# A hybrid transformer block on one core: the second tokens' first output projection placed in attention's last steps, operands formed in PSUM

## Chip, core and metric

The kernel runs on one core of a Trainium2 chip. The metric is the device time of one execution in microseconds. The span in a profile is the time from its first to its last instruction.

## The reference

One block over 1024 tokens of width 1024. An RMSNorm and one input projection feed a pooling mixer (512 columns) and differential attention (four heads of two score maps each, block-causal). Their outputs are put side by side, projected by `w_o` and added to x. A second RMSNorm feeds a gated MLP (up projection to 2 x 2816 columns, causal convolution of width 3 over the tokens, silu(gate) x value, down projection), which is added, and a last RMSNorm follows.

```python
mix = jnp.concatenate([pool_out, attn_out], axis=-1) @ w_o[l]
x = x + mix
h = rmsnorm(x, norm_ffn_g[l])
u = causal_dwconv(h @ w_up[l], conv_w[l], conv_b[l])
gate, val = jnp.split(u, 2, axis=-1)
x = x + (jax.nn.silu(gate) * val) @ w_down[l]
...
return rmsnorm(x, norm_final_g)
```

## The kernel before

Tokens lie in eight tiles of 128 (`tt` 0 to 7). The first tokens are tiles 0 to 3, the second tokens 4 to 7. Every float32 operand of a large product is split into a high part, rounded by ScalarE (`split`, L86), and a low part, the rest, by VectorE or GpSimd (L87). A product is then three matmuls, `mm3` (L79 to L81): high by high, high by low, low by high.

The start. `col` holds columns of constants, among them the norm's gain. For each of eight k tiles a weight tile `wv` and a tile of the transposed input `xT` are loaded by the SP queue and split, and the value projection `pv` is formed in all eight PSUM banks.

Attention. `att_steps` makes a list of steps, 32 query tiles and 8 steps to finish, and `merge` weaves units from the list `fill` between them, among them the output projection of the first tokens. A fifth entry of a unit in `fill` names the step at which it comes at the latest.

The output projection. `wo_part(hf, part, n)` loads and splits weights for one token half, one half of the rows of `w_o` (`part` 0 holds the pooled columns, `part` 1 the attention's) and one half of the output columns. `wo_unit(tt, part, n, w)` is twelve matmuls into a bank `po` and one addition into `X1[tt]` on VectorE.

The second norm. `norm2a(tt)` squares and sums `X1[tt]` on ScalarE, makes the inverse root on GpSimd, and multiplies on VectorE by it and by the gain `gb`, which SP loads, into `xn`. `norm2b(tt)` transposes `xn` on TensorE into a PSUM tile `t` of two banks: `q1` (first four k tiles) and `q2`.

The up projection follows Winograd's form of Strassen's product, seven half-size products in place of eight. The right operands are blocks of the transposed tokens: B11 and B21 (first tokens), B22 (second tokens' `q2`), and the sums T1 = B12 - B11, T2 = B22 - T1, T3 = B22 - B12, T4 = B21 - T2, with B12 = `q1` of the second tokens. The left operands are weight blocks a11 to a22 and their sums S1 to S4, made on GpSimd from loads. `operand` gives their places, `osplit` splits into them. The first four units of the up projection (`AHEAD`) have their products P1 (with B11) and P2 (with B21) done ahead, while the second tokens' operands are made; `ug`, by `c11`, is the addition on VectorE that follows P2. Then the loop `up` begins with P6, the product of S2 and T2, then Z, of S1 and T1. Later pages of the program, the convolution and the down projection, have an order written out by hand for all engines (from `manual_schedule`); before that a scheduler at build time orders each engine's instructions by their priority in the code, and `tc.high_priority()` puts some of them forward.

The end. The last product group is finished tile by tile: `evac` adds it to X on VectorE, `last1` squares on ScalarE, applies the gain on VectorE, forms the mean on GpSimd (`mean`) and the inverse root there (`power`), and `last2` multiplies one half on VectorE and one on ScalarE and stores each half.

Of the kernel before, what the change touches and what calls it, by code (L numbers as in the profile page):

```python
# [50 lines left out]
def block_kernel(ctx, tc, x, xT, pos, wv, wqk, wp, wo, wup, wdn, cols, invf, rcnt, gffn, gfin,  # L51
# [58 lines left out]
    nc.sync.dma_start(out=col[:, 0:16], in_=cols[:, 0:16])  # L110
# [33 lines left out]
    pv = []  # L144
    for i in range(2):
        s = psS(f"pv{i}")
        pv += [s[:, 0:H], s[:, H:T]]
    for i in range(4):
        pv.append(psB(f"pv{4 + i}"))
# [485 lines left out]
    def norm2b(tt):  # L635
# [11 lines left out]
        t1, t4 = fb["B11", tt - 4], fb["B21", tt - 4]  # L647
        sub = ALU.subtract
# [12 lines left out]
        fb["B22", tt] = b22  # L661
# [15 lines left out]
    w00 = wo_part(1, 0, 0, "s")  # L677
# [242 lines left out]
    for u in us[:AHEAD]:  # L920
# [7 lines left out]
        if u.n == 0:
            norm2b(7)
# [313 lines left out]
```

## Time and profile before

| what | us |
|---|---|
| median of three runs | 1042.85 |
| lowest of them | 1039.86 |
| the profiled execution | 1039.9 |
| its span | 1038.1 |
| TensorE busy in the span | 1009.8 |
| VectorE busy | 765.1 |
| ScalarE busy | 508.0 |
| GpSimd busy | 246.5 |

One of the three runs took 2449.37 us and tells nothing about the kernel. The profile's times count from the span's start. PE is TensorE, PEld its weight loads, DVE VectorE, ACT ScalarE, POOL GpSimd, SP the queue that issues the transfers. In a row of a timeline the bracket holds the idle time of the engine just before the instruction and what ended it.

### The profile page before, as it was taken

The numbers are of one execution on the slowest core, as the hardware profiler recorded it, in microseconds if no ns is written. First come the engines' busy times: TensorE is split into PE (matmuls) and PEld (weight loads), VectorE is DVE, ScalarE is ACT, GpSimd is POOL, SyncE is SP. The second block draws the span as 40 slices with busy tenths as digits, with TensorE's granted clock in tenths as the row PEclk, the third lists the DMA queues.
The fourth block names the chain that finished last, engine by engine and source line by source line (L and its number), as shares of the span: only waits on it lengthen the run. The fifth ranks groups of instructions, "written<-read, shape, count | busy, mean of one in ns | idle before, by whom it ended". The sixth has DMA issues, their size and how long they took to land.

```text
span 1038.1 us, 13407 instructions
## 1 busy us (share of the span) xinstructions
PE 1009.8 (97%) x4612; PEld 834.6 (80%) x4612; DVE 765.1 (74%) x1169; ACT 508.0 (49%) x884; POOL 246.5 (24%) x232
## 2 busy tenths in 40 slices
PE   8999999998998999999999999999999999999997
PEld 6888888886887887778888888888888788888885
DVE  6466777989775869688876776776776878958774
ACT  6732554447554545353544545445445453544553
POOL 0000112223221137543333332432432000000221
PEclk9999999999999999999999999999999999999999
DMA  9627543324325412223331431432321897533342
GB/s 313 240 87 257 194 163 112 109 70 148 102 81 186 150 61 72 101 92 112 132 117 56 140 113 51 143 112 72 132 102 41 297 389 266 173 111 101 120 145 81
DMA packets 67971, 143.88 MB, mean 139 GB/s; under 512 B 8512, under 2 KB 9664, under 8 KB 67904
## 3 DMA queue, kind: packets, MB, share of 16 engines
q1 hardware_dynamic: 67904, 143.03, 39.9%
q8 instruction: 36, 0.59, 0.2%
q14 instruction: 31, 0.25, 0.1%
HBM read 105.78 MB, written 37.22 MB: 138 GB/s over the span
## 4 chain that ended last, share of the span: by engine, by line
PE 73%; DVE 7%; issue 2%; ACT 2%; DMA 1%; POOL 1%; SPq 1%; POOLq 0%; DVEq 0%; ACTq 0%
PE P L81 8%; PE P L79 8%; PE P L80 8%; PE Z L79 3%; PE x L80 3%; PE x L81 3%; PE Z L81 3%; PE Z L80 3%; PE x L79 3%; PE dP L79 3%; PE dP L81 3%; PE dP L80 3%; PE po L81 3%; PE po L79 3%; PE po L80 3%; PE sc L386 3%
## 5 line engine op out<-in xcount | busy, mean ns | idle before, releaser
L403 POOL TENSOR_SCALAR e<-e,sm 128x128 f32<-128x128 f32 (+7 forms) x32 | 29.9, 936 | 175.8 <-DMA k<-tsk 69.5
L735 POOL TENSOR_TENSOR S<-wa,wa 128x512 f32<-128x512 f32 x44 | 64.8, 1495 | 0.5 <-DMA wa<-in_wup 0.5
L399 ACT ACTIVATE e<-sc,mx 128x128 f32<-128x128 f32 (+7 forms) x64 | 47.2, 742 | 32.2 <-DVE mx L389 16.7
L1034 POOL TENSOR_SCALAR s<-s 128x1 f32<-128x1 f32 x12 | 9.4, 786 | 212.8 <-ACT sq0None L1031 167.5
L753 DVE SCALAR_TENSOR_TENSOR o<-ug,col,o 128x1023 f32<-128x1023 f32 (+1 forms) x44 | 56.4, 1282 | 0.0
L753 DVE SCALAR_TENSOR_TENSOR o<-uv,col,o 128x1023 f32<-128x1023 f32 (+1 forms) x44 | 56.3, 1280 | 0.0
L735 POOL TENSOR_TENSOR S<-S,wa 128x512 f32<-128x512 f32 x22 | 28.3, 1287 | 73.8 <-DVE a227l L87 4.8
L860 ACT COPY u<-P 128x512 f32<-128x512 f32 x18 | 10.6, 590 | 69.2 <-PE P L81 69.2
L386 PE MATMUL sc<-K,Q 128*128 128x512 f32 (+3 forms) x192 | 42.6, 351 | 0.7 <-ACT e L399 0.7
L735 POOL TENSOR_TENSOR S<-wa,S 128x512 f32<-128x512 f32 x22 | 28.5, 1295 | 50.5 <-issue 50.4
L386 PEld LDWEIGHTS sc<-K,Q 128*128 128x128 f32 x192 | 32.4, 189 | 6.0 <-ACT e L399 1.2
L421 ACT COPY at<-tp 128x512 f32<-128x512 f32 (+3 forms) x48 | 21.6, 483 | 28.8 <-PE tp L417 28.8
L748 ACT ACTIVATE o<-ug,col 128x1024 f32<-128x1024 f32 x22 | 26.7, 1212 | 18.2 <-DVE ug L912 18.2
L840 ACT COPY u<-P 128x512 f32<-128x512 f32 x18 | 10.6, 590 | 49.9 <-PE P L81 49.9
L433 PE MATMUL O<-at,V 128*128 128x256 f32 (+1 forms) x160 | 34.0, 358 | 0.0
L433 PEld LDWEIGHTS O<-at,V 128*128 128x128 f32 x160 | 29.8, 190 | 4.0
L816 DVE TENSOR_TENSOR ac<-o,g 128x1024 f32<-128x1024 f32 x22 | 26.9, 1225 | 7.9 <-ACT g L814 7.9
L389 DVE TENSOR_REDUCE mx<-sc 128x1 f32<-128x640 f32 (+3 forms) x32 | 32.3, 1016 | 0.4
L564 DVE TENSOR_TENSOR X<-X,po 128x512 f32<-128x512 f32 x32 | 21.7, 683 | 13.6 <-PE po L81 13.5
L748 ACT ACTIVATE o<-uv,col 128x1024 f32<-128x1024 f32 x22 | 26.7, 1213 | 9.1 <-DVE uv L892 9.1
L814 ACT ACTIVATE g<-o 128x1024 f32<-128x1024 f32 x22 | 22.7, 1030 | 13.6 <-DVE o L753 13.5
L879 ACT COPY s<-P 128x512 f32<-128x512 f32 x18 | 10.6, 590 | 32.8 <-PE P L81 32.8
(2451 smaller groups left out, 3479.9 us busy)
## 6 DMA issues: line engine op xcount, KB each, us to landing
wa<-in_wup SPq DMA_DIRECT2D x88, 256.0 KB, 3.2
S<-s SPq DMA_DIRECT2D x22, 512.0 KB, 2.9
arP<-S SPq DMA_DIRECT2D x44, 256.0 KB, 2.6
arP<-A SPq DMA_DIRECT2D x33, 256.0 KB, 4.5
Q<-q SPq DMA_DIRECT2D x64, 128.0 KB, 2.8
A<-ac SPq DMA_DIRECT2D x11, 512.0 KB, 2.8
xs<-in_x SPq DMA_DIRECT2D x8, 512.0 KB, 8.0
K<-k SPq DMA_DIRECT2D x8, 512.0 KB, 4.9
```

Of the source, the lines that this page charges most:

```text
L79: mm(dst, lhi, rhi, start=first, stop=False, skip_group_check=more)
L80: mm(dst, lhi, rlo, start=False, stop=False, skip_group_check=more)
L81: mm(dst, llo, rhi, start=False, stop=last, skip_group_check=more)
L386: mm(sc[:, k0:k1], qst[h, grp][n * 2 + hl][:, qc], kst[h][n][:, k0:k1], start=hl == 0, stop=hl == 1)
L389: nc.vector.tensor_reduce(out=nmx[:, n:n + 1], in_=sc[:, 0:L], axis=AX.X, op=ALU.max, negate=True)
L399: nc.scalar.activation(ee[n], scs[n][:, 0:L], AF.Exp, bias=nmx[:, n:n + 1], accum_out=sums[:, n:n + 1])
L403: nc.gpsimd.tensor_scalar(out=e1, in0=e1, scalar1=sums[:, 3:4], scalar2=1.0, op0=ALU.mult, op1=ALU.mult)
L433: mm(O[:, c0:256], V[j][:, h * P:(h + 1) * P], at[:, j, c0:256], start=j == 0, stop=j == nj - 1)
L735: pool(out=t, in0=getattr(u, x), in1=getattr(u, y), op=op)
L748: nc.scalar.activation(o, src, AF.Identity, bias=col[:, cc + 3:cc + 4], scale=col[:, cc + 2:cc + 3])
L753: nc.vector.scalar_tensor_tensor(out=o[:, d:T], in0=src[:, 0:T - d], scalar=col[:, cc + 2 - d:cc + 3 - d], in1=o[:, d:T], op0=ALU.mult, op ...
L816: tens(out=p.act, in0=p.o1, in1=g, op=ALU.mult)
```

## The change

Four things are changed.

1. At the start `col` and the first quarter of the first `xT` tile are issued by ScalarE instead of SP, the second `xT` tile comes in halves, and TensorE first multiplies a tile of zeros seven times into a bank that the first real product overwrites.
2. The second tokens' first output projection (`part` 0, first column half) becomes four units of `fill`, due at the steps 35 to 38 of 40, with its weights and the loads of the second tokens' X in the first of them. Before, it was written behind the attention, each unit ahead of a `norm2a`.
3. For the second tokens `norm2b` no longer makes T1 and T2 in SBUF. VectorE writes T1 over `q1` and T2 over `q2`; B22 is split from `q2` at once, not later by another loop; T4's subtraction moves from GpSimd to VectorE. The `norm2b` of tiles 4 to 7 come at other places.
4. At the end the mean is no longer a GpSimd instruction: its factor is in the square's scale, and VectorE adds the constant. `last2` splits a tile at column 640, not 512, and stores it whole.

```diff
 col = cst.tile([P, 192], F32, name="col")
-nc.sync.dma_start(out=col[:, 0:16], in_=cols[:, 0:16])
+nc.scalar.dma_start(out=col[:, 0:16], in_=cols[:, 0:16])
...
+zero = st("lo", "zero")
+nc.vector.memset(zero, 0.0)
+zr = st("hi", "zeror", dt=F32R)
+nc.vector.tensor_copy(out=zr, in_=zero)
+for i in range(7):
+    mm(pv[7], zr[:, 0:P], zr, start=True, stop=True)
...
+    t = st("E", f"xT{kt}")
+    w = 256 if kt == 0 else H if kt == 1 else T
+    if kt == 0:
+        nc.scalar.dma_start(out=t[:, 0:w], in_=xT[0:P, 0:w])
...
+w00 = []
+def wo_first(tt):
+    if not w00:
+        load_x1(1)
+        w00.extend(wo_part(1, 0, 0, "s"))
+    wo_unit(tt, 0, 0, w00)
+    yield
+fill += [(wo_first(4 + j), 0.0, 35 + j, 0.0, 35 + j) for j in range(4)]
...
-t1, t4 = fb["B11", tt - 4], fb["B21", tt - 4]
-nc.vector.tensor_tensor(out=t1, in0=q1, in1=t1, op=sub)
+b1, t4 = fb["B11", tt - 4], fb["B21", tt - 4]
+sub, tens = ALU.subtract, nc.vector.tensor_tensor
 b22 = st("Q", f"B22f{tt}", [P, 4, P])
 nc.scalar.copy(out=b22, in_=q2)
-t2 = st("T", f"T2f{tt}", [P, 4, P])
-nc.gpsimd.tensor_tensor(out=t2, in0=b22, in1=t1, op=sub)
 t3 = st("Q", f"T3f{tt}", [P, 4, P])
-nc.vector.tensor_tensor(out=t3, in0=b22, in1=q1, op=sub)
-osplit("T1", tt, t1)
-osplit("T2", tt, t2)
-osplit("T3", tt, t3)
-nc.gpsimd.tensor_tensor(out=t4, in0=t4, in1=t2, op=sub)
+tens(out=t3, in0=b22, in1=q1, op=sub)
+tens(out=q1, in0=q1, in1=b1, op=sub)
+osplit("B22", tt, q2)
+tens(out=q2, in0=b22, in1=q1, op=sub)
+tens(out=t4, in0=t4, in1=q2, op=sub)
+osplit("T2", tt, q2)
+osplit("T1", tt, q1)
+osplit("T3", tt, t3, None)
 osplit("T4", tt, t4, nc.gpsimd)
-fb["B22", tt] = b22
...
-w00 = wo_part(1, 0, 0, "s")
...
-for tt in range(4, 8):
-    wo_unit(tt, 0, 0, w00)
-    if tt < 6:
-        norm2a(tt - 4)
+norm2a(0)
+norm2a(1)
...
-    nc.scalar.activation(junk[:, cs], X[tt][:, cs], AF.Square, accum_out=...)
+    nc.scalar.activation(junk[:, cs], X[tt][:, cs], AF.Square, scale=1.0 / 32, accum_out=...)
...
-    mean(s[:, 3:4], s[:, 0:1], s[:, 2:3])
+    tens(out=s[:, 3:4], in0=s[:, 0:1], in1=s[:, 2:3], op=add)
...
-    for n in range(2):
-        emit(tt, halves[n])
+    m = 640
...
+    emit(tt, slice(0, T))
```

The order of the instructions is the scheduler's, and changes at the start, between the end of attention and P6, and at the end; SP's is the same but for the start and the stores at the end, and from P6's first matmul to the last product TensorE's is the same.

On ScalarE at the start of the program before (`g08` are gains of the attention's norm, made from `col`):

```order
L338 ACT_TABLE_LOAD
L338 ACTIVATE g08_483<-col_69 128x4
L86 CAST wv0h_75<-wv0r_73 128x512
L89 ACTIVATE hTh0_71<-xT0_79,col_69 128x256 x4
L86 CAST wv1h_94<-wv1r_92 128x512
```

and now:

```order
L110 DMA col_69<-in_cols 128x16
L139 DMA xT0_90<-in_xT 128x256
L86 ACT_TABLE_LOAD
L86 CAST wv0h_94<-wv0r_92 128x512
L349 ACTIVATE g08_497<-col_69 128x4
L89 ACTIVATE hTh0_88<-xT0_90,col_69 128x256 x4
L86 CAST wv1h_112<-wv1r_110 128x512
```

The two issues come first, and `g08` moved behind the cast of the first weight tile.

On TensorE where attention ends, before (`rb` and `so` are small steps of the heads' norm, `t20` and `t21` the transposes of token tiles 0 and 1, `po004` the product of tile 4):

```order
L456 MATMUL rb23_3169<-ident_168,rs23_3099 128x128 x2
L638 MATMUL t20_3423<-ident_168,xn0_3263 128x128 x4
L638 MATMUL t21_3467<-ident_168,xn1_3286 128x128 x4
...
L444 MATMUL so33_3175<-ones_173,sq33_3158 128x1 x2
L456 MATMUL rb32_3183<-ident_168,rs32_3164 128x128 x2
L456 MATMUL rb33_3187<-ident_168,rs33_3178 128x128 x2
L79 MATMUL po004_3249<-wo100h_3205,cat010_2293 128x512
L80 MATMUL po004_3249<-wo100l_3206,cat010_2293 128x512
L81 MATMUL po004_3249<-wo100h_3205,cat011_2294 128x512
```

and now:

```order
L467 MATMUL rb23_3183<-ident_188,rs23_3113 128x128 x2
L79 MATMUL po004_3221<-wo100h_3199,cat010_2307 128x512
L80 MATMUL po004_3221<-wo100l_3200,cat010_2307 128x512
...
L81 MATMUL po004_3221<-wo103h_3217,cat011_2308 128x512
L658 MATMUL t20_3437<-ident_188,xn0_3319 128x128 x4
L658 MATMUL t21_3481<-ident_188,xn1_3328 128x128 x3
L79 MATMUL po005_3235<-wo100h_3199,cat010_2307 128x512
...
L455 MATMUL so33_3249<-ones_193,sq33_3172 128x1 x2
L658 MATMUL t20_3437<-ident_188,xn0_3319 128x128 x4
L658 MATMUL t21_3481<-ident_188,xn1_3328 128x128 x5
L467 MATMUL rb32_3257<-ident_188,rs32_3178 128x128 x2
L79 MATMUL po006_3261<-wo100h_3199,cat010_2307 128x512
```

Twelve matmuls of tile 4, and then of tile 5, moved ahead of the transposes and of the small steps that stood in front of them.

On VectorE at the last token tile's operands, before (`ug...` is the addition after P2 of one unit, `S20l` the low part of the first unit's S2):

```order
L649 TENSOR_TENSOR B11f3_3547<-t27_3824,B11f3_3547 128x512
L655 TENSOR_TENSOR T3f7_3838<-B22f7_3834,t27_3824 128x512
L87 TENSOR_TENSOR T110_3646<-B11f3_3547,T100_3645 128x4x128
L742 TENSOR_TENSOR ug11_3905<-P211_3892,s111_3890 128x512
L87 TENSOR_TENSOR T310_3655<-T3f7_3838,T300_3653 128x2x128
L87 TENSOR_TENSOR T311_3656<-T3f7_3838,T301_3654 128x2x128
L87 TENSOR_TENSOR T210_3650<-T2f7_3836,T200_3649 128x4x128
L742 TENSOR_TENSOR ug1_3935<-P21_3922,s11_3920 128x512
L742 TENSOR_TENSOR ug12_3965<-P212_3952,s112_3950 128x512
L87 TENSOR_TENSOR S20l_3968<-S20_3863,S20h_3967 128x512
```

and now (L674 writes T1 into `t27`, L676 T2, L677 is T4):

```order
L673 TENSOR_TENSOR T3f7_3869<-B22f7_3867,t27_3858 128x512
L674 TENSOR_TENSOR t27_3858<-t27_3858,B11f3_3561 128x512
L87 TENSOR_TENSOR T310_3687<-T3f7_3869,T300_3685 128x2x128
L87 TENSOR_TENSOR T311_3688<-T3f7_3869,T301_3686 128x2x128
L87 TENSOR_TENSOR B2210_3672<-t27_3858,B2200_3671 128x4x128
L676 TENSOR_TENSOR t27_3858<-B22f7_3867,t27_3858 128x512
L677 TENSOR_TENSOR B21f3_3565<-B21f3_3565,t27_3858 128x512
L759 TENSOR_TENSOR ug12_3975<-P212_3962,s112_3960 128x512
L87 TENSOR_TENSOR T210_3678<-t27_3858,T200_3677 128x4x128
L87 TENSOR_TENSOR S20l_3978<-S20_3913,S20h_3977 128x512
L87 TENSOR_TENSOR S10l_3982<-S10_3909,S10h_3981 128x512
L87 TENSOR_TENSOR T110_3682<-t27_3858,T100_3681 128x4x128
```

The two subtractions for T2 and T4 and B22's split came into VectorE's row; T1's low part (`T110`) moved from the third place to behind S2's and S1's, and T2's (`T210`) stands behind `ug12`, no longer ahead of it.

## Rows read from the trace of the kernel before

**Rows 1.** page, part 1: busy us, share of the span, instructions of each engine
```profile
PE 1009.8 (97%) x4612; PEld 834.6 (80%) x4612; DVE 765.1 (74%) x1169; ACT 508.0 (49%) x884; POOL 246.5 (24%) x232
```

**Rows 2.** table by stage: stretch; its us; busy us (x) of five engines; clock; DMA
```profile
330.00:340.00 10.00, 6.41 (x36) 4.63 (x35) 7.46 (x19) 5.97 (x13) 1.81 (x3) 0.89 0.64 215
...
340.00:350.00 10.00, 10.00 (x43) 8.18 (x42) 9.53 (x16) 7.24 (x14) 3.10 (x4) 0.94 0.42 152
...
400.00:410.00 10.00, 7.80 (x34) 6.10 (x33) 9.35 (x15) 4.97 (x11) 4.89 (x4) 0.98 0.31 106
...
410.00:420.00 10.00, 7.63 (x26) 5.54 (x25) 6.98 (x6) 3.91 (x7) 9.12 (x7) 0.85 0.27 92
...
480.00:600.00 120.00, 120.00 (x531) 99.36 (x530) 86.73 (x101) 58.72 (x89) 44.81 (x33) 1.00 0.31 106
...
1020.00:1038.10 18.10, 10.69 (x48) 8.51 (x46) 7.20 (x12) 5.47 (x12) 3.46 (x8) 0.89 0.31 116
```

**Rows 3.** timeline, start of the span: start us, us, engine, line, operation, idle before
```profile
0.73 0.39 SPq L110 DMA_DIRECT2D col<-in_cols  x1
...
1.17 0.42 SPq L96 DMA_DIRECT2D wv0r<-in_wv  x1
...
2.39 0.21 ACT L338 ACTIVATE g<-col 128x4 f32<-128x4 f32 x1 [0.39 <-DMA col<-in_cols]
...
4.04 0.62 ACT L86 CAST wv0h<-wv0r 128x512 fp32r<-128x512 f32 x1 [1.45 <-DMA wv0r<-in_wv]
...
5.12 0.79 PE L79 MATMUL pv<-wv0h,hTh 128*128 128x512 f32 x1 [5.12 <-ACT hTh L89]
...
9.56 0.63 PE L79 MATMUL pv<-wv0h,hTh 128*128 128x512 f32 x1
...
9.98 0.48 PE L80 MATMUL pv<-wv0l,hTh 128*128 128x512 f32 x1
```

**Rows 4.** timeline around the end of attention, TensorE and VectorE
```profile
330.52 0.41 PE L456 MATMUL rb<-ident,rs 128*128 128x128 f32 x2
...
331.71 1.42 DVE L617 SCALAR_TENSOR_TENSOR xn<-X,r,gbhi 128x512 f32<-128x512 f32 x2 [3.31 <-DMA gbhi<-in_gffn]
...
338.46 0.78 PE L79 MATMUL po<-wo100h,cat 128*128 128x512 f32 x1
...
350.79 0.39 PE L79 MATMUL po<-woh,cat 128*128 128x512 f32 x1
```

**Rows 5.** instructions by form, 378 to 420 us: count | busy, mean ns | idle before, releaser
```profile
L87 DVE TENSOR_TENSOR T<-T2f,T 128x512 fp32r<-128x512 f32 x4 | 4.3, 1074 | 0.0
...
L655 DVE TENSOR_TENSOR T3f<-B22f,t 128x512 f32<-128x512 f32 x4 | 2.7, 682 | 1.3 <-ACT B22f L651 1.3
...
L653 POOL TENSOR_TENSOR T2f<-B22f,B11f 128x512 f32<-128x512 f32 x4 | 5.9, 1470 | 10.1 <-ACT B22f L651 10.1
...
L651 ACT COPY B22f<-t 128x512 f32<-128x512 f32 x4 | 2.4, 588 | 13.2 <-DVE B11f L649 13.2
```

**Rows 6.** timeline, operands of the last token tile and what follows on TensorE
```profile
398.83 0.66 PE L638 MATMUL t<-ident,xn 128*128 128x128 f32 x4 [0.35 <-DVE xn L617]
...
405.18 0.68 DVE L649 TENSOR_TENSOR B11f<-t,B11f 128x512 f32<-128x512 f32 x1
...
408.05 0.50 PE L79 MATMUL P<-B,aa120h 128*128 128x512 f32 x1 [2.20 <-ACT s L924]
...
417.26 0.50 PE L79 MATMUL P<-T,S20h 128*128 128x512 f32 x1 [1.85 <-ACT S20h L86]
```

**Rows 7.** timeline of the last token tile; then DMA issues: count, KB, us to landing
```profile
1032.33 0.34 POOL L1034 TENSOR_SCALAR s<-s 128x1 f32<-128x1 f32 x1 [1.07 <-ACT sq L1031]
...
1033.34 0.72 ACT L1084 ACTIVATE of<-of,s 128x512 f32<-128x512 f32 x1 [0.49 <-POOL s L1037]
...
out_dram<-of SPq DMA_DIRECT2D x4, 512.0 KB, 2.9
out_dram<-of SPq DMA_DIRECT2D x8, 256.0 KB, 2.2
```

More of the change, by code (lines that the diff above doesn't have):

```diff
@@ L109, in block_kernel @@
     col = cst.tile([P, 192], F32, name="col")
-    nc.sync.dma_start(out=col[:, 0:16], in_=cols[:, 0:16])
+    nc.scalar.dma_start(out=col[:, 0:16], in_=cols[:, 0:16])
+    pv = []
+    for i in range(2):
+        s = psS(f"pv{i}")
+        pv += [s[:, 0:H], s[:, H:T]]
+    for i in range(4):
+        pv.append(psB(f"pv{4 + i}"))
+    zero = st("lo", "zero")
[4 more added lines that the diff above has]
+        mm(pv[7], zr[:, 0:P], zr, start=True, stop=True)
     hT = [[None] * NK, [None] * NK]
@@ L121, in block_kernel @@
         hT[1][kt] = b[:, kt % 2, :]
+        t = st("E", f"xT{kt}")
+        w = 256 if kt == 0 else H if kt == 1 else T
+        if kt == 0:
+            nc.scalar.dma_start(out=t[:, 0:w], in_=xT[0:P, 0:w])
         wvs.append(weight(wv[:, kt, :], f"wv{kt}"))
-        t = st("E", f"xT{kt}")
-        w = 256 if kt == 0 else T
         for c0 in range(0, T, w):
             c = slice(c0, c0 + w)
-            nc.sync.dma_start(out=t[:, c], in_=xT[kt * P:(kt + 1) * P, c])
+            if kt or c0:
+                nc.sync.dma_start(out=t[:, c], in_=xT[kt * P:(kt + 1) * P, c])
             split(t[:, c], hT[0][kt][:, c], hT[1][kt][:, c], col[:, kt:kt + 1])
@@ L141, in block_kernel @@
     nc.sync.dma_start(out=rcn, in_=rcnt.partition_broadcast(P))
[L144 to L149, printed above, removed]
     for kt in range(NK):
@@ L695, in block_kernel @@
         wo_unit(tt, 1, 0, w10)
+        if tt > 5:
+            norm2b(tt - 2)
         wo_unit(tt, 1, 1, w11)
         norm2a(tt)
-        if tt > 4:
-            norm2b(tt - 1)
     acts, opd, U = {}, {}, {}
@@ L924, in block_kernel @@
         nc.scalar.copy(out=u.s1, in_=x)
+        if u.n < 2:
+            norm2b(6 + u.n)
         y = psB(f"P2{u.f}")
@@ L927, in block_kernel @@
         c11(u, y)
-        if u.n == 0:
-            norm2b(7)
+        if u.n == 1:
+            u = us[0]
             up_load(u, "a21", "a22", "a11", "a12")
@@ L932, in block_kernel @@
                 up_sum(u, k)
-            for tt in range(4, 8):
-                osplit("B22", tt, fb["B22", tt], nc.gpsimd if tt % 2 else None)
     up_split(us[0], "S2")
@@ L1030, in square @@
         junk = psS(f"sq{tt}{n}")
-        nc.scalar.activation(junk[:, cs], X[tt][:, cs], AF.Square, accum_out=s3[tt][:, n or 0:(n or 0) + 1])
-    def mean(dst, src, plus):
-        nc.gpsimd.tensor_scalar(out=dst, in0=src, scalar1=1.0 / D, scalar2=plus, op0=ALU.mult, op1=ALU.add)
+        nc.scalar.activation(junk[:, cs], X[tt][:, cs], AF.Square, scale=1.0 / 32, accum_out=s3[tt][:, n or 0:(n or 0) + 1])
     def power(s):
@@ L1049, in upper @@
         elif step == 1:
-            mean(s[:, 3:4], s[:, 0:1], EPS)
+            nc.vector.tensor_scalar_add(out=s[:, 3:4], in0=s[:, 0:1], scalar1=EPS)
             power(s[:, 3:4])
@@ L1070, in lower @@
         elif step == 1:
-            mean(s[:, 2:3], s[:, 1:2], EPS)
+            nc.vector.tensor_scalar_add(out=s[:, 2:3], in0=s[:, 1:2], scalar1=EPS)
             gain(tt, 1)
@@ L1082, in last2 @@
         o, s = fin[tt], s3[tt]
-        nc.vector.tensor_scalar_mul(out=o[:, 0:H], in0=o[:, 0:H], scalar1=s[:, 3:4])
-        nc.scalar.activation(o[:, H:T], o[:, H:T], AF.Copy, scale=s[:, 3:4])
-        for n in range(2):
-            emit(tt, halves[n])
+        m = 640
+        nc.vector.tensor_scalar_mul(out=o[:, 0:m], in0=o[:, 0:m], scalar1=s[:, 3:4])
+        nc.scalar.activation(o[:, m:T], o[:, m:T], AF.Copy, scale=s[:, 3:4])
+        emit(tt, slice(0, T))
     todo = {}
```

2 lines of the change are left out of this document (removed).

## The prediction

> **What bounds the kernel now.** The line of engines [rows 1] comes first: TensorE is busy for 1009.8 us of 1038.1 and no other engine reaches 75%. So an edit away from TensorE is worth only what it takes out of the 28.3 us in which TensorE stands still, or out of the stretches where its clock is halved. The table by stage [rows 2] says where these are: from 480 to 600 us TensorE is busy 120.00 of 120.00 (531 matmuls, 0.226 us each) and nothing there can be won by overlap. The losses that the diff touches are four. Ahead of the first matmul 5.12 us pass [rows 3]. Around 330 to 350 us, where attention ends and the output projection of the second tokens begins (I call it the join), 3.59 us are idle and the granted clock is 0.89 and 0.94, which is another 0.11 x 10 + 0.06 x 10 = 1.7 us of full-speed time. Around 400 to 420 us, where the up projection's operands are made, 2.20 + 2.37 us are idle and the clock is 0.98 and 0.85, another 0.2 + 1.5 = 1.7 us. In the last stretch TensorE is busy 10.69 of 18.10 us, so 7.4 us follow its last matmul. The whole loss in reach is 5.1 + 5.3 + 6.3 + 7.4 us plus a slow start, and I take the four places in turn. The sum is made against the profiled execution's 1039.9 us, which is the lowest of the three times shown and 2.95 us under their median.
>
> **The start.** The chain is: SP issues `col` at 0.73 and `wv0r` at 1.17; the cast of `wv0r` begins at 4.04, 2.87 us after its issue; hTh follows and the first matmul starts at 5.12 [rows 3]. With `col` and the first piece of xT issued by ScalarE, `wv0r` takes SP's first place, 0.44 us earlier. But the new order on ScalarE puts the small g08 activation (0.21 us) between that cast and hTh, where it stood ahead of the cast before; and ScalarE's two issues come ahead of its table load, which still ends well before the weights land. So the first real matmul moves by 0.44 - 0.21 = 0.2 us, to 4.9. The larger part is the clock. The matmuls that start at 9.56 and 9.98 are 0.42 us apart, against 0.226 us later: the array starts at its lower level (1.2 GHz) although this column prints 1.00 there, and it stays there for about 4.9 us from the first matmul. Eleven matmuls start in that time, each 0.2 us too long. The seven products of zeros need a memset and a cast of 128x512 on VectorE, which does nothing else before 4 us; I estimate that they begin at 1.8 us and last 7 x 0.43 = 3.0 us, so they end where the real work begins and cost nothing. If the rise again comes 4.9 us after the first product, at 6.7, four real matmuls are slow instead of eleven: 7 x 0.2 = 1.4. Together **1.6 us**. Ends: 0.2 if the zeros don't raise the clock, 2.4 if no real matmul is slow. Data keeps up, since xT's second block is cut into halves and the next weights are issued two places earlier on SP.
>
> The start's clock has its page too: the Trainium skill (TensorE: Matmul & The Clock Gate, Part 1: The HAM clock gate) says that the phase of the activity watch is free, so that the number of slow matmuls at a start differs from run to run. No run here shows that; by it the term could be anything between its two ends, and the sum would move by about 1 us.
>
> **The join.** TensorE makes rb at 330.52 and then wants the transposes of xn, which VectorE can't form until gbhi has landed (its idle 3.31 us, until 331.71) [rows 4]; small steps that wait for each other follow, the first product of the second tokens starts at 338.46, already at the half clock (0.63 us), and the products with the second column half start at 350.79. The new order puts the twelve products of token tile 4 directly behind rb, those of tile 5 behind seven transposes, and the norm's small steps between them. A group of twelve takes 12 x 0.226 = 2.7 us, more than the time from rb to the end of VectorE's wait, and their weights are the ones loaded before the join. SP's order is the same on both sides there, so gbhi lands no later. What takes the wait's place: each group's PSUM buffer is freed by VectorE's addition, and VectorE holds the splits of `wor` in the same order; following it row by row I find tile 7's group waiting at worst 0.7 us for the addition of tile 5. From rb's end (330.93) to 350.79 are 19.9 us, in which stand 48 products (10.9 us) and, as I estimate, 2.3 us of transposes and small ones: 6.7 us over. The windows give 5.3. I take 6.2, the middle of the two rounded up, less the 0.7 us of new wait: **5.5 us** (4.0 to 6.3).
>
> Costed at nothing: the second tokens' X loads (same place on SP), and the last head's `cat`, now split some 10 us after rb but still about 2.5 us ahead of its first product; if that cover is gone, the excess falls on TensorE.
>
> **The operands.** What changes hands for each of the four token tiles: T2f, the update of B21f and half of B22's low parts leave GpSimd: 4 + 4 + 2 instructions, the shortest kind of which has a mean of 1470 ns [rows 5], so about 15 us. VectorE takes them at some 0.68 us, the mean of T3f, which reads PSUM as they do: 4 x 0.68 + 4 x 0.68 + 2 x 0.68 = 6.8 us more. In return the T2 and T1 splits, 1074 ns from SBUF now, would be at T3f's 0.68: 8 x 0.39 = 3.2 us less. The in-place PSUM results have no row; I take T3f's price, with 0.6 and 1.1 as ends. Before, VectorE came to the last tile at 405.18, some 6 us after its transposes (398.83), and from there came the idle spells: 2.20 us before 408.05, where a product waits for ScalarE, and 1.85 us before 417.26 [rows 6]. With less slowed work I get VectorE to the last tile some 2 us after its transposes.
>
> The transposes of tile 7 now stand later on TensorE, 27 matmuls (6.1 us) ahead of the product that needs T2. VectorE's row for tile 7 is T3f, q1, two half splits, B22, q2, T4 (about 4.5 us with the 2 us of lag and some contention: 7 to 8), then ug12, which waits for the last of those 27 matmuls, and only then T2's low part and S20l, another 2 x 0.68. So the wait at P6 doesn't vanish; I put it at 2.8 us. Old loss 6.3, new 2.8, leaves **3.5 us** (0 to 5). A new wait that is queued too: the t buffers are held until T1 is split, so the transposes of tiles 6 and 7, and all matmuls behind them, wait for VectorE's splits of tiles 4 and 5; I find 3 us or more of cover.
>
> ScalarE's copy of B22f stood 13.2 us in four times behind VectorE's subtraction on the other half of the same PSUM tile [rows 5]: the two engines take turns on it. The Trainium skill (PSUM — Partial Sum Buffer, PSUM bank collisions raise a hardware error) has a rule for this: two engines may not use one bank at a time and must be ordered. That speaks against forming more in PSUM: copy, T3f and q1, cast, split, q2 and T4, cast, split, cast, split become one chain of turns, 7 x 0.68 + 0.59 + 3 x 0.62 = 7.2 us a tile. After the last transposes T2 would then be ready after 5.9 us and T1 after 7.2; TensorE wants them 6.1 and 8.8 us after. By the rule the sum stays within 1 us of mine, as long as VectorE isn't behind.
>
> **The end.** Four instructions follow each last addition; the GpSimd step at 1032.33 (0.34 us) becomes a small VectorE addition and the last ScalarE multiplication (0.72 us at 1033.34) becomes 384 wide [rows 7]: 0.3 + 0.1 us, and one issue less. Against it one 512 KB store lands in 2.9 us where 256 KB take 2.2, and VectorE now multiplies tile 6 after that addition. **0.3 us** (-0.5 to 0.9).
>
> **Sum.** 1.6 + 5.5 + 3.5 + 0.3 = 10.9; 1039.9 - 10.9 = **1029.0 us**. Between the stages TensorE is full and its order is unchanged, so a shift passes through.
>
> **Rivals.**
> - Operand stage bound by VectorE: its share is already 9.35 of 10 us at 400 to 410 us [rows 2]. If splits there stay at 1.07 us, the wait at P6 grows to 5 us or more, the clock falls again (1.7), and nothing of the 3.5 is won: 1039.9 - 7.4 = 1032.5. For it: 13 VectorE instructions a tile. Against: T3f's 682 ns beside a busy GpSimd. Chance 0.2.
> - Zeros don't warm the array: the change does not do there what it seems to. 1039.9 - 9.5 = 1030.4. Chance 0.1.
> - Everything at its good end (2.4 + 6.3 + 5 + 0.9): 1025.3. Chance 0.07.
> - Slower than before: PSUM results in place cost VectorE far more than T3f. There are 28 such instructions (7 a tile) in one queue, ahead of ug and S20l, which TensorE waits for. Cover and gain are 3 + 11 us, so it decides from 0.68 + 14/28 = 1.2 us each; at 1.4 us the time is 1039.9 + 6 = 1046. No row has such a price. Chance 0.03.
>
> **How the numbers follow.** My forecast has the remaining 0.6. With the ends of the terms and some 2 us for a median above the lowest run, 1023.5 to 1036 holds a bit over 8 in 10. Two per cent is 20.9 us, about what a measurement of this kernel can tell from no change; only the slow cases of the old median, or a gain past all four good ends, get there: faster 0.03, within 0.95, slower 0.02.
>
> **What would show it.** Products 0.226 us apart from about 7 us; twelve products of tile 4 directly behind rb near 329 us, at full clock; the first product with T2 near 405 us with one wait of 2 to 3 us at S20l or T2; GpSimd near idle from 370 to 395 us. I am wrong if the join only moves its idle time to the groups of tiles 6 and 7, or if VectorE's PSUM rows exceed 1 us.

## The result and the profile after

The changed kernel takes 1030.9 us (median of six, 1028.8 to 1031.9) where the kernel before takes 1042.99 us (median of six): a ratio of 0.989, 95% interval 0.987 to 0.9911, or 12.1 us less. One of the six runs of before took 2449.37 us and tells nothing; without it their median is 1042.85 us and the difference 11.95. A second measurement of both gave 1029.83 against 1042.21 us, 0.9882 (0.9863 to 0.99). The profiled execution took 1028.8 us, its span is 1027.0 us.

The page's line of engines, which answers to [rows 1]: GpSimd has lost 25.6 us of work, and VectorE, which took most of it over, is not busier.

```profile
PE 1008.2 (98%) x4619; PEld 834.1 (81%) x4619; DVE 763.9 (74%) x1194; ACT 506.2 (49%) x885; POOL 220.9 (22%) x210
```

The table by stage of the changed kernel, for the stretches of [rows 2] (stretch, its length, busy us of the five engines, granted clock, DMA share). Since all work comes earlier, the operand stage now ends in the third row and not in the fourth. The join is nearly full (0.25 us idle) and at full clock. In the operands 2.4 us are idle and the clock of that stretch is 0.83, another 0.17 x 10 = 1.7 us.

```profile
330.00:340.00 10.00, 10.00 (x55) 8.12 (x53) 9.27 (x18) 3.98 (x8) 0.71 (x1) 1.00 0.62 223
340.00:350.00 10.00, 9.75 (x47) 8.00 (x47) 8.91 (x19) 9.35 (x19) 2.30 (x5) 1.00 0.41 132
400.00:410.00 10.00, 7.60 (x27) 5.37 (x26) 8.63 (x10) 5.36 (x11) 7.36 (x6) 0.83 0.37 130
410.00:420.00 10.00, 10.00 (x46) 8.29 (x45) 4.47 (x7) 1.21 (x2) 3.47 (x3) 1.00 0.17 57
```

The timeline at the start of the changed kernel, for [rows 3]. The zeros run from 1.90 to 5.25, as sized. The weight tile's cast starts only 0.27 us earlier than before, the first real matmul 0.22 us later. But only the first two or three are slow.

```profile
1.90 3.35 PE L124 MATMUL pv<-zeror 128*128 128x512 f32 x7 [1.90 <-DVE zeror L122]
...
3.77 0.62 ACT L86 CAST wv0h<-wv0r 128x512 fp32r<-128x512 f32 x1 [0.84 <-DMA wv0r<-in_wv]
...
5.34 0.79 PE L79 MATMUL pv<-wv0h,hTh 128*128 128x512 f32 x1
5.93 0.62 PE L80 MATMUL pv<-wv0l,hTh 128*128 128x512 f32 x1
6.36 0.43 PE L79 MATMUL pv<-wv0h,hTh 128*128 128x512 f32 x1
6.63 0.40 PE L80 MATMUL pv<-wv0l,hTh 128*128 128x512 f32 x1
```

The timeline of TensorE at the join, for [rows 4]. Tile 4's products stand directly behind rb; of the waits for VectorE's additions 0.25 us are left; the second column half begins at 343.34.

```profile
328.86 0.41 PE L467 MATMUL rb<-ident,rs 128*128 128x128 f32 x2
329.03 0.48 PE L79 MATMUL po<-wo100h,cat 128*128 128x512 f32 x1
...
340.31 0.50 PE L79 MATMUL po<-wo100h,cat 128*128 128x512 f32 x1 [0.25 <-DVE X L575]
...
343.34 0.48 PE L79 MATMUL po<-woh,cat 128*128 128x512 f32 x1
```

The forms of VectorE in the operand stage of the changed kernel (count | busy, mean ns | idle before), for [rows 5]: splits and sums that read PSUM take the 0.68 to 0.69 us that T3f takes, where the split of T2f from SBUF took 1.07.

```profile
L87 DVE TENSOR_TENSOR T<-t,T 128x512 fp32r<-128x512 f32 x8 | 5.5, 684 | 1.6 <-ACT T L86 1.6
...
L676 DVE TENSOR_TENSOR t<-B22f,t 128x512 f32<-128x512 f32 x4 | 2.8, 692 | 0.1
L674 DVE TENSOR_TENSOR t<-t,B11f 128x512 f32<-128x512 f32 x4 | 2.8, 692 | 0.0
```

And the timeline of the last tile, for [rows 6], in order of start: VectorE reaches it at 398.68, 2.4 us after its transposes (396.31) and not some 6; its two half splits of T3 stand beside GpSimd's sums; ScalarE waits with T2's cast behind VectorE's turn on the bank, and casts B21f and S20h only then; TensorE waits for S20h.

```profile
398.68 0.68 DVE L673 TENSOR_TENSOR T3f<-B22f,t 128x512 f32<-128x512 f32 x1
...
399.88 1.85 DVE L87 TENSOR_TENSOR T<-T3f,T 128x256 fp32r<-128x256 f32 x2
...
403.81 0.58 ACT L86 CAST T<-t 128x512 fp32r<-128x512 f32 x1 [2.37 <-DVE B21f L677]
...
404.81 0.62 ACT L86 CAST S20h<-S 128x512 fp32r<-128x512 f32 x1
...
405.48 0.56 PE L79 MATMUL P<-T,S20h 128*128 128x512 f32 x1 [2.01 <-ACT S20h L86]
406.87 0.80 PE L81 MATMUL P<-T,S20l 128*128 128x512 f32 x1 [0.39 <-DVE S20l L87]
```

The tail of the changed kernel, for [rows 7]: the GpSimd mean (0.34 us) is a VectorE addition of 0.16, the last ScalarE multiplication takes 0.62 in place of 0.72, but the inverse root on GpSimd takes 0.79 where it took 0.55 before (the second fence, from the kernel before).

```profile
1021.40 0.16 DVE L1092 TENSOR_TENSOR s<-s 128x1 f32<-128x1 f32 x1
...
1021.64 0.79 POOL L1051 TENSOR_TENSOR s<-s,nhalf 128x1 f32<-128x1 f32 x1 [1.28 <-DVE s L1092]
1022.47 0.62 ACT L1099 ACTIVATE of<-of,s 128x384 f32<-128x384 f32 x1 [0.59 <-POOL s L1051]
```

```profile
1032.76 0.55 POOL L1037 TENSOR_TENSOR s<-s,nhalf 128x1 f32<-128x1 f32 x1
```

### The profile page after: what moved, and what is told of

It reads as the page before. It is cut to its first block, busy times and chain, and to the rows that moved or that the text cites. A ratio compares the mean times of both kernels' runs of the same rounds, so it can differ in the third digit from the quotient of the medians.

```text
span 1027.0 us, 13420 instructions
## 1 busy us (share of the span) xinstructions
PE 1008.2 (98%) x4619; PEld 834.1 (81%) x4619; DVE 763.9 (74%) x1194; ACT 506.2 (49%) x885; POOL 220.9 (22%) x210
## 4 chain that ended last, share of the span: by engine, by line
PE 77%; DVE 3%; DMA 3%; ACT 1%; issue 1%; SPq 0%; POOL 0%; POOLq 0%; DVEq 0%; ACTq 0%
PE P L81 9%; PE P L79 9%; PE P L80 9%; PE Z L79 4%; PE Z L80 4%; PE Z L81 4%; PE x L80 3%; PE x L81 3%; PE x L79 3%; PE dP L79 3%; PE dP L80 3%; PE dP L81 3%; PE po L81 3%; PE po L79 3%; PE po L80 3%; PE sc L397 3%
## 5 line engine op out<-in xcount | busy, mean ns | idle before, releaser
L1051 POOL TENSOR_TENSOR s<-s,nhalf 128x1 f32<-128x1 f32 x8 | 7.8, 979 | 221.0 <-DVE s L1064 182.1
L575 DVE TENSOR_TENSOR X<-X,po 128x512 f32<-128x512 f32 x32 | 21.6, 681 | 10.9 <-PE po L81 10.7
```

## The experiments

My theory was the sum of the prediction: four terms, nearly independent, of which the join is the largest and the operands the one with a wait left at P6. The rivals: the start's gain is the loads' order; the join's gain is given back later; the operands' gain comes from the transposes' places. A single execution's time scatters by some us, so the stages are compared by four marks of one profile of each kernel, read from each kernel's timeline: the rb of [rows 4] (`rb23` in the orders above), the first product of the second column half, the first of the ahead products (on `aa00h`), and the first Z. The last column is the time from the last addition into X to the span's end. Times in us.

| kernel | rb at | rb to second half | ahead products to Z | last addition to end |
|---|---|---|---|---|
| before | 330.52 | 20.27 | 33.93 | 7.37 |
| e_start | 328.41 | 20.51 | 35.91 | 7.42 |
| e_join | 330.79 | 14.78 | 35.48 | 7.43 |
| e_oper | 330.58 | 22.28 | 31.10 | 7.43 |
| e_psum | 330.19 | 21.87 | 31.34 | 7.40 |
| e_order | 329.58 | 19.06 | 36.66 | 7.32 |
| changed | 328.86 | 14.48 | 30.56 | 7.12 |
| after_again (changed) | 330.73 | 14.67 | 31.08 | 7.11 |
| n0 | 330.23 | 14.19 | 30.75 | 7.10 |
| p6_dummies | 328.75 | 14.80 | 29.52 | 7.11 |
| t2_first | 329.39 | 14.69 | 29.83 | 7.09 |
| s2_first | 329.21 | 14.63 | 30.55 | 7.15 |
| sums_early | 328.58 | 14.55 | 28.85 | 7.10 |
| p6_all | 329.40 | 14.89 | 27.74 | 7.11 |

**The start alone** (e_start): the kernel before with the diff's hunks on the start.

```diff
+    nc.scalar.dma_start(out=col[:, 0:16], in_=cols[:, 0:16])
...
+    for i in range(7):
+        mm(pv[7], zr[:, 0:P], zr, start=True, stop=True)
```

> The kernel before with the start's edits alone (zeros, the two ScalarE loads, the halves of the second xT tile). Theory: the whole of the shift of rb, 330.52 to 328.86, comes from the start, so rb stands at 328.9 here, the products with the second column half at 349.1 and Z at 419.3, each 1.6 to 1.7 us earlier than before, and the time is 1.6 us lower. Rival: the join waits for something that the start does not move (the gain's load, VectorE's splits), and takes a part back: rb at 328.9, but the second column half at 350 or later, and a time less than 0.8 us lower.

Measured: 1040.05 against 1042.51 us, ratio 0.9978 (0.9968 to 0.9988), 2.5 us less. rb stands at 328.41, the second half at 348.92, as the theory says: the join takes nothing back. The time fell by more than the 1.6 us of the theory, which its interval (1.2 to 3.3 us) holds. But Z is at 421.07, not 419.3, since in this execution the wait at P6 was 3.40 us with a longer spell of lower clock (0.75 in 410:420).

**The start without the zeros** (n0): the changed kernel less their products.

```diff
-    for i in range(7):
-        mm(pv[7], zr[:, 0:P], zr, start=True, stop=True)
```

> The changed kernel without the seven products of zeros; everything else of the start stays. Theory: the zeros carry the start's gain by the clock, the loads' new order only the rest. The first real matmul stands at 4.9 to 5.0, products are 0.42 us apart for almost 5 us from there, the second k tile's first matmul is at 12.6 (11.43 with the zeros, 12.84 before) and rb at 330.0 (328.86 and 330.52). Rival: the loads' order carries it: the second k tile's first matmul at 11.4 or earlier.

Measured (one run, 1030.44 us, within the range of the changed kernel's): first real matmul at 5.26, the second k tile's first matmul at 12.82, rb at 330.23, 1.4 us later than in the changed kernel's first profile. The five kernels with the old start have rb at 329.58 to 330.79, 330.33 on average. So no gain of the loads' new order is shown (330.23 lies within that range), and as far as these profiles show the gain is that of the zeros; the first real matmul is not at 4.9 with or without them. What the zeros change is when the spacing falls under 0.3 us: at 7.95 to 10.89 in the six profiles without them, at 5.77 to 7.34 in seven of the eight with them.

The changed kernel's second profile (after_again, below) is the eighth, with the same instructions: the zeros end at 5.25, the weights land late, the array stands 0.52 us, and products stay 0.43 us apart until 9.78.

```profile
5.77 0.80 PE L79 MATMUL pv<-wv0h,hTh 128*128 128x512 f32 x1 [0.52 <-ACT hTh L89]
...
9.35 0.63 PE L79 MATMUL pv<-wv0h,hTh 128*128 128x512 f32 x1
9.78 0.46 PE L80 MATMUL pv<-wv0l,hTh 128*128 128x512 f32 x1
10.08 0.40 PE L79 MATMUL pv<-wv0h,hTh 128*128 128x512 f32 x1
```

In the eight profiles with the zeros rb is at 328.41 to 330.73, 329.17 on average: 1.2 us earlier than with the old start. The Trainium skill (TensorE: Matmul & The Clock Gate, Part 1: The HAM clock gate) says that the phase of the activity watch is free, so that the number of slow matmuls varies between runs. These profiles agree: the full spacing begins at 6.36 and at 10.08 in two profiles of the one changed kernel.

**The join alone** (e_join): the kernel before with the four units in `fill`.

```diff
+    fill += [(wo_first(4 + j), 0.0, 35 + j, 0.0, 35 + j) for j in range(4)]
...
-    for tt in range(4, 8):
-        wo_unit(tt, 0, 0, w00)
```

> The kernel before with the first output projection of the second tokens moved into attention's steps, and nothing else. Theory: rb stays at 330.5, the twelve products of tile 4 stand behind it, the second column half begins 5.8 us earlier (345.0), the operand stage loses its 6.3 us as before, so Z is at 415.1 and the time 5.5 to 5.8 us lower. Rival: the operand stage is paced by GpSimd and VectorE and not by TensorE, so it waits longer when TensorE comes early: Z at 417 or later, the time at most 4 us lower.

Measured: 1036.24 against 1042.51 us, ratio 0.9942 (0.9926 to 0.9959), 6.3 us less. rb to the second half falls from 20.27 to 14.78. Z is at 417.48, where the rival had put it, but not by its mechanism: the waits of the operand stage are the old ones to 0.03 us (2.17, 1.87 and 0.52 against 2.20, 1.85 and 0.52 [rows 6]); what is longer is the spell of lower clock behind them (0.83 in 400:410, 0.98 before). The time of four runs, 1036.15 to 1037.22, speaks for the theory.

**The operands alone** (e_oper): the hunks on `norm2b`, on its places and on the low parts of B22.

```diff
+        tens(out=q1, in0=q1, in1=b1, op=sub)
+        osplit("B22", tt, q2)
+        tens(out=q2, in0=b22, in1=q1, op=sub)
...
+        if tt > 5:
+            norm2b(tt - 2)
```

> The kernel before with the operand stage's edits alone (sums in PSUM, the later places of the transposes of tiles 4 to 7, no separate low parts of B22). Theory: the second column half begins at 350.8 as before, Z 3.2 us earlier (417.8), with one wait of about 2 us ahead of P6 and a spell of lower clock behind it; the time is 3.2 us lower. Rival: the operand edits pay only because the join's edit brought the transposes forward; then Z stays within 1.5 us of 420.9.

Measured: 1037.67 against 1042.51 us, ratio 0.9953 (0.9938 to 0.9968), 4.8 us less, more than the 3.2 of the theory. Z is at 420.17, not at 417.8 and within the rival's 1.5 us of 420.9; but that is since the second half begins at 352.86 and not at 350.8. The stage itself has one wait of 2.01 us at P6 and 0.66 at S20l, and 31.10 us from the ahead products to Z, as in the changed kernel, though the join's edit was absent: the rival's mechanism falls, though its sign came true. The second half is late by the clock: the table by stage of e_oper, and then that of the kernel before, show the old join in two executions with the same work. Of 330:340 TensorE is busy 6.53 and 6.41 us, but the granted clock (the column before the DMA share) is 0.50 and 0.52, almost all at the lower level, 1.2 GHz, against 0.79 and 0.87.

```profile
335.00:340.00 5.00, 3.65 (x17) 3.12 (x16) 3.91 (x14) 5.00 (x11) 1.40 (x2) 0.50 0.53 158
340.00:345.00 5.00, 5.00 (x14) 3.88 (x13) 3.37 (x7) 4.10 (x8) 0.00 (x0) 0.52 0.44 136
```

```profile
335.00:340.00 5.00, 3.02 (x14) 2.30 (x13) 4.17 (x15) 5.00 (x12) 1.41 (x2) 0.79 0.55 171
340.00:345.00 5.00, 5.00 (x21) 4.03 (x20) 4.53 (x8) 4.44 (x8) 0.00 (x0) 0.87 0.42 149
```

**Sums without the new places** (e_psum) and **places without the sums** (e_order). The first keeps the transposes' old places:

```diff
+        tens(out=q2, in0=b22, in1=q1, op=sub)
...
-            for tt in range(4, 8):
-                osplit("B22", tt, fb["B22", tt], nc.gpsimd if tt % 2 else None)
```

> The kernel before with the sums formed in PSUM (and B22's low parts there), but the transposes of tiles 4 to 7 in their old places. Theory: the sums carry the operand stage's gain, since ten slow GpSimd instructions go; from the first ahead product to Z at most 32 us (33.9 to 35.9 before, 31.1 with the later transposes too), and the wait of 2.2 us at the fourth unit's products is gone. Rival: the gain is that of the places; then 33.5 us or more, with VectorE's row waited for at the fourth unit as before.

The second forms the operands as before, on GpSimd, in the new places:

```diff
+        if u.n < 2:
+            norm2b(6 + u.n)
...
-        if u.n == 0:
-            norm2b(7)
+        if u.n == 1:
+            u = us[0]
```

> The kernel before with the transposes of tiles 4 to 7 in the later places, and the operands formed as before (T2 and the update on GpSimd). Theory: with GpSimd's 1.47 us steps in the chain of tile 7 and its transposes later, P6 waits longer than before: 4 us or more in place of 1.9 to 3.4; from the first ahead product to Z 34 us or more. Rival: the places carry the gain: 32 us or less.

Measured: e_psum 31.34 us from the ahead products to Z (1038.28 us, one run), with the wait at the fourth unit gone and 2.28 + 0.66 us left; e_order 36.66 us (1040.26 us, one run). So the sums in PSUM carry the gain, and the new places alone bring none (33.93 to 35.91 us with the old ones). Each edit holds one thing more, which no run takes apart: that of e_psum puts ScalarE's copy of B22 ahead of VectorE's first subtraction, and that of e_order, like the whole change, makes the first unit's sums S1 to S4 one unit later. From the timeline of e_order, first GpSimd, then VectorE, then ScalarE and TensorE:

```profile
405.54 1.30 POOL L653 TENSOR_TENSOR T2f<-B22f,B11f 128x512 f32<-128x512 f32 x1 [3.72 <-ACT B22f L651]
406.80 1.74 POOL L87 TENSOR_TENSOR B<-B22f,B 128x512 fp32r<-128x512 f32 x1
408.50 1.45 POOL L659 TENSOR_TENSOR B21f<-B21f,T2f 128x512 f32<-128x512 f32 x1
...
414.23 1.26 POOL L735 TENSOR_TENSOR S<-S,wa 128x512 f32<-128x512 f32 x1
...
407.31 2.93 DVE L87 TENSOR_TENSOR T<-T3f,T 128x256 fp32r<-128x256 f32 x2
410.16 1.75 DVE L87 TENSOR_TENSOR T<-T2f,T 128x512 fp32r<-128x512 f32 x1
...
415.51 0.62 ACT L86 CAST S20h<-S 128x512 fp32r<-128x512 f32 x1 [2.93 <-POOL S L735]
...
416.18 0.79 PE L79 MATMUL P<-T,S20h 128*128 128x512 f32 x1 [6.98 <-ACT S20h L86]
```

What ends P6's wait there is not the last tile's T2, whose split is done at 411.91, but the sum S2 (`S<-S,wa`), which GpSimd makes only behind its work for the token tiles. In the kernel before it is the same wait: the cast of S20h at 416.59 stands 2.99 us for that sum, and P6 at 417.26 for the cast [rows 6].

```profile
415.30 1.26 POOL L735 TENSOR_TENSOR S<-S,wa 128x512 f32<-128x512 f32 x1
...
416.59 0.62 ACT L86 CAST S20h<-S 128x512 fp32r<-128x512 f32 x1 [2.99 <-POOL S L735]
```

In the changed kernel the same sum ends at 401.44, and the cast at 404.81 waits for it no longer:

```profile
400.10 1.34 POOL L752 TENSOR_TENSOR S<-S,wa 128x512 f32<-128x512 f32 x1
```

VectorE and GpSimd also slow each other in e_order: VectorE's splits from SBUF take 1.75 and 2 x 1.47 us for the 0.68 and 2 x 0.38 that they take alone in other rows of this kernel. In the changed kernel only S20l, S10l and T3's halves are so slowed (1.35, 1.76, 1.85 for two), while sums and splits that read PSUM stay at 0.68 to 0.70 beside a busy GpSimd. The Trainium skill (SBUF — State Buffer, Who interferes with whom) says that a VectorE instruction with two SBUF inputs contends with a GpSimd instruction that reads SBUF, and that one with at most one SBUF input, outside VectorE's two-port modes, does not; these rows agree.

**Who sets P6** (t2_first, s2_first): in the changed kernel either T2's split goes ahead of the update of B21f for the last tile, or S2's split is put forward.

```diff
+        if tt == 7:
+            osplit("T2", tt, q2)
         tens(out=t4, in0=t4, in1=q2, op=sub)
```

> The changed kernel with tile 7's T2 split put ahead of the update of B21f. Theory: the cast of T2 is held by the turn, not by VectorE's result q2, which is there at 403.05; it starts at 403.1 in place of 403.81, S20h stands directly behind it (403.6) and P6 starts at 404.3 with a wait of 0.9 us. Rival: P6's end is set by VectorE's row up to S20l; then the wait only moves from the first product to the third, which still starts at 406.5 or later.

```diff
-            for k in (1, 3, 2, 4):
+            for k in (1, 2, 3, 4):
                 up_sum(u, k)
-    up_split(us[0], "S2")
+            with tc.high_priority():
+                up_split(u, "S2")
```

> The changed kernel with the sum S2 made before S3 and its split put forward, so that ScalarE casts S20h and S10h in its idle time at 401.4 to 403.8, ahead of T2's cast. Theory: P6's first product then starts with T2's cast, at 404.5, and S20l is no longer waited for; but VectorE now has S20l and S10l ahead of T2's low part, so the second product waits for that instead, until about 406, and Z comes no more than 0.6 us earlier at the same clock. Rival: the place of S20h on ScalarE is the whole cause, VectorE has room; then P6 has one wait of 1.1 us, and none behind it.

Measured, TensorE's waits in t2_first and then in s2_first:

```profile
405.00 0.50 PE L79 MATMUL P<-T,S20h 128*128 128x512 f32 x1 [0.78 <-ACT S20h L86]
...
407.93 0.50 PE L81 MATMUL P<-T,S20l 128*128 128x512 f32 x1 [2.20 <-DVE S20l L87]
```

```profile
405.04 0.51 PE L79 MATMUL P<-T,S20h 128*128 128x512 f32 x1 [1.07 <-ACT T L86]
...
406.82 0.79 PE L80 MATMUL P<-T,S20h 128*128 128x512 f32 x1 [1.28 <-DVE T L87]
```

Both mechanisms are as I said (T2's cast waits 1.66 us for the sum itself and no longer for B21f; S20h no longer waits), and neither helps: the wait moves to the third product, as the rival had it, or to the second, and grows to 2.98 us or stays at 2.35 (2.40 in the changed kernel). That t2_first's stage is 0.7 us shorter all the same (29.83) comes from the clock, which stayed at 1.00 in its profile. VectorE's row is the end that counts.

**Working through the wait** (p6_dummies): eight products into P6's own bank, which its first real product overwrites.

```diff
+            if u.n == 0:
+                d = opnd["B11"][0][0]
+                for _ in range(8):
+                    mm(x6, d[:, 0, 0:P], d[:, 0, :], start=True, stop=True)
```

> The changed kernel with eight products of B11 by itself put into the bank of P6 ahead of P6, whose first product overwrites them: TensorE works through the wait in place of standing still. Theory: the fall of the clock after the changed kernel's wait (0.83 of 400:410) comes from the idle time alone, and is a price of its own. P6's real products start at 405.5 as before, since S20h comes no earlier, the third waits 0.4 us for S20l, but all are 0.226 us apart; Z at 408.6 in place of 410.33, the granted clock of 400:410 is 1.00 and the time 13.5 to 14 us under the kernel before (12.1 without them). Rival: the clock falls for another reason, or the 0.4 us at S20l are enough; then Z stays at 410 or later.

Measured: 1028.21 against 1040.76 us, ratio 0.9879 (0.9858 to 0.99), 12.6 us less. The clock stays at 1.00; Z comes 29.52 us after the ahead products began, 1.0 us sooner than in the changed kernel's first profile and not 1.7, since S20l is now waited for 0.66 us where the slow products hid part of it. That the eight products kept the clock up is not shown by this one profile, since it also stayed at 1.00 behind the real waits of t2_first and sums_early; and the time shows no gain over the changed kernel (0.9879 of before against 0.989 and 0.9882). The real products start no earlier:

```profile
403.52 1.97 PE L844 MATMUL P<-B 128*128 128x512 f32 x8
405.69 0.50 PE L79 MATMUL P<-T,S20h 128*128 128x512 f32 x1 [0.20 <-ACT S20h L86]
407.09 0.50 PE L81 MATMUL P<-T,S20l 128*128 128x512 f32 x1 [0.66 <-DVE S20l L87]
```

**The sums earlier** (sums_early): loads, sums and S2's split of the first unit one unit earlier, with t2_first's edit.

```diff
-        if u.n == 1:
-            u = us[0]
+        if u.n == 0:
             up_load(u, "a21", "a22", "a11", "a12")
```

> The changed kernel with the loads and sums of S1 to S4 of the first unit one unit earlier (where the kernel before has them), S2's split behind them, and tile 7's T2 split ahead of the update of B21f. Theory: S20h and S20l are done before tile 7; P6 starts with T2's cast, at 403.8, its second product with T2's low part, at 404.5: waits of 1.1 us together in place of 2.4. Z at 409.0 if the clock falls as in the changed kernel, 407.4 if it stays up; the time 1.3 to 2.9 us under the changed kernel's, 13.4 to 15 under the kernel before. Rival: VectorE is the bound here, and S20l and S10l ahead of the last tiles push its whole row back: T3f of tile 7 starts 1.3 us or more behind 398.68, and P6 still waits 2 us or more.

Measured: 1028.11 against 1040.76 us, ratio 0.988 (0.9851 to 0.9909). Half of each account: T3f of the last tile starts at 400.49, 1.8 us later (VectorE also stands 1.47 us for S20h), and P6 waits 1.78 + 0.23 us, as the rival said, in place of the theory's 1.1; the clock stayed up and the stage took 28.85 us. The time is 12.6 us under the kernel before and not 13.4 to 15, so no gain over the changed kernel is shown in it.

**A version meant to beat both** (p6_all): sums_early, T2 and T1 of the last tile ahead of the low parts of B22 and of the update, and four products ahead of P6; beside it the changed kernel again.

```diff
+        if tt == 7:
+            tens(out=t4, in0=t4, in1=q2, op=sub)
+            osplit("B22", tt, b22)
...
+                for _ in range(4):
+                    mm(x6, d[:, 0, 0:P], d[:, 0, :], start=True, stop=True)
```

> A version that should beat both kernels: the sums of the first unit one unit earlier, as in the run with the early sums; for tile 7, T2 and T1 formed and split ahead of the low parts of B22 (made from the copy in SBUF) and of the update of B21f; and four products of B11 by itself ahead of P6 to fill what is left. Theory: VectorE's row is the end that counts; T2's cast moves from 404.4 to about 403.6, TensorE works up to 404.2, P6 waits 0 to 0.4 us, the clock stays at 1.00. From the first ahead product to Z 28.3 to 28.6 us (changed kernel 30.56, early sums 28.85); the time 1.8 to 2.5 us under the changed kernel's on the same chip. Rival: TensorE's wait is not all of it, VectorE's later work (the splits of T3, B22 and the update moved behind) delays P7 or the products behind it; then Z comes early and the gain is gone by 430.

> The changed kernel itself, beside the version that should beat it. From the first ahead product to Z 30.5 to 31.1 us (two waits of 2.4 to 2.7 us together, and 0 to 2 us of lower clock), from rb to the second column half 14.2 to 14.8, and a time 12 us under the kernel before.

Measured on one chip: p6_all 1026.59 us (1025.89 to 1027.23), ratio to before 0.9857 (0.984 to 0.9873); the changed kernel 1029.83 us (1027.19 to 1031.43); before 1042.21 us. The stage takes 27.74 us, less than the 28.3 to 28.6 expected, P6 waits 0.23 us, and from Z to the last addition it is 609.53 us against 609.59: nothing is given back. The medians are 3.2 us apart, where 1.8 to 2.5 was expected. Three of the four executions of p6_all are faster than all five of the changed kernel, though the intervals of the two ratios overlap. Which of its three edits carries the gain was not taken apart. The rows of p6_all:

```profile
404.26 1.07 PE L849 MATMUL P<-B 128*128 128x512 f32 x4
405.83 0.50 PE L80 MATMUL P<-T,S20h 128*128 128x512 f32 x1 [0.23 <-DVE T L87]
```

## Why the prediction was right

The forecast was 1029.0 us, the median 1030.9; the gain was 12.1 us against 10.9. The single parts' medians add up to 2.5 + 6.3 + 4.8, with 0.3 for the end 13.9; their intervals (some 1 us to either side for the start, 1.6 for the others) hold the difference from 12.1, so no exchange between the parts is shown or excluded. The two profiled executions, each the lowest of its kernel's six runs here, lie 11.1 us apart, and the four terms measured between them are 1.7, 5.8, 3.2 and 0.3.

- **The base.** The sum was made against an execution of 1039.9 us, 3 us under the median; I called this scatter. So 1029.0 was in effect a forecast for a low execution (1028.8 was the lowest), not for the median. The old join takes 19.06 to 22.28 us in five profiles (20.27 in that of before) with the same work: TensorE stands still for 3.0 to 3.7 us in all five, and the rest of the difference is its busy time, 16.0 to 18.9 us, by how long the clock is low. The change takes the low clock out of the join and shortens it at the start, so it gains more on average than against that one execution: by the means below 1.2 + 6.2 + 4.0 + 0.3 = 11.7. That the rest of the 12.1 comes from the same is likely, but not shown.
- **The start**, 1.6: the step "0.44 earlier, so 4.9" failed. The weights were issued 0.45 us earlier and their cast started 0.27 us earlier in the first profile, 0.12 us later in the second; the first real matmul stands at 5.34 to 5.77 with the zeros. In the first profile rb moved by 1.66 us although the first real matmul came 0.22 later, so the clock gave 1.9 and not 1.4: the sum of 1.6 held there by two misses that cancel, which is luck. In the second profile the zeros gave nothing. On average rb moved by 1.2 us.
- **The join**, 5.5: the mechanism held to the row. Against the profiled execution the piece shrank by 5.8 us, over all profiles by 20.8 - 14.6 = 6.2 (means of five and nine). The new wait that I put at 0.7 us at worst was 0.25 there, 0.5 to 0.69 in seven others and absent in n0. The 6.2 of the sum is not the middle of 5.3 and 6.7, which is 6.0; it came nearer by this slip.
- **The operands**, 3.5: VectorE's price of 0.68 us for in-place sums, the lag of some 2 us and a wait at S20h of 2.8 (2.01 + 0.39 measured) held. What the likeliest case left out was the fall of the clock behind the wait (1.7), which I had given to the VectorE rival alone. But the old loss was too small as well: TensorE's work in this stage takes 26.85 us at full clock (t2_first: 29.83 with 2.98 of waits), so the loss was 33.93 - 26.85 = 7.1 us and not 6.3, the new one 3.7 and not 2.8. The difference held because both were short by nearly the same, which is luck. And the prediction names only half of the old path to P6: VectorE came late to the last tile, but from there GpSimd took over, which started T2f at 406.55 after 4.32 us of waiting and worked without a break until S2 was made at 416.56 (above). Taking its instructions away freed S2, which the prediction does not count. Three old stages average 35.1 us, four of the changed kind (changed twice, n0, e_oper) 30.9. The stretch from the second half to the ahead products grew by 0.2 us (36.21 to 36.43), so 4.0 remain. "GpSimd near idle" was wrong: it is busy 3.77 of 10 us in 380:390 with T4's low parts, and its sums at 400 slow VectorE. The 13.2 us of the copy [rows 5] were no matter of one bank: it reads `q2` and the subtraction `q1`, two banks of the tile. With the copy put first in the code (e_psum) ScalarE stood 3.7 us in the four, all for the transposes.
- **The end**, 0.3: 7.40 us on average in the six old ends, 7.11 in the eight new ones. The inverse root on GpSimd cost 0.24 us more than before; the steps on either side made up for it.

Of the rivals, zeros that don't warm the array happened in one profile of eight; the VectorE-bound stage happened in its place (the row that sets P6 is VectorE's), but at the changed kernel's 0.68 us and not at 1.07.

## What to carry to other kernels

A profile shows one draw of the clock: where TensorE waits some 2 us, compare stages over several profiles by marks in the program before trusting a difference of 1 or 2 us. A wait that can't be removed can be worked through with products into a bank that is overwritten anyway; the clock stayed at 1.00 in both profiles in which this was done, though what it is worth in time by itself is not shown. And when a wait names an engine, reorder that engine's row only after asking which other row ends next: at P6 two correct edits each moved the wait to a later product and made it no shorter.

## What was not expected of the hardware

The clock did not fall after every wait of the same size. Behind the 2.01 us at P6 it fell in four profiles of four, to 0.83 of 400:410 in the changed kernel, and behind 1.07 and 1.28 us in s2_first, each time at a cost of 1.7 us by the granted clock; behind 2.20 us in t2_first and 1.78 us in sums_early it stayed at 1.00. A wait of 2.17 us at the fourth unit's products was followed by a fall in e_join (0.83 in 400:410) and by none in e_start (1.00). So the length of the wait alone does not decide; what does was not tried.

GpSimd's inverse root of 128x1 took 0.55 us in the kernel before. In the changed kernel it took 0.55 us for the first of the last four tiles, after 34.87 us of idle time, and 0.79 us for the other three, in each of which VectorE's multiplication of 128x640 runs beside it; so it is in all eight profiles with the new end. In the kernel before, that multiplication (128x512) ran beside the mean, which took 0.32 to 0.34 us with it and 0.27 without. That VectorE slows GpSimd here is argued from these rows; no run takes the multiplication away.

```profile
1015.47 0.55 POOL L1051 TENSOR_TENSOR s<-s,nhalf 128x1 f32<-128x1 f32 x1 [34.87 <-DVE s L1092]
...
1021.48 0.55 DVE L1098 TENSOR_SCALAR of<-of,s 128x640 f32<-128x640 f32 x1
```
